# Hybrid decoder layer, down projection: banks copied by ScalarE, residual sums spread over the steps, activation combinations formed earlier; keys scaled once in the recurrence

## The chip, the cores and the metric

The kernel runs on one core of one Trainium2 chip. The metric is the device time of one launch in microseconds, as the median of several runs. One more execution is recorded by the hardware profiler; the views below come from that one.

## The reference

One layer of a hybrid decoder trunk, sequence 1024, model width 1024, all float32:

```python
h = rmsnorm(x, norm1_w)
proj = h @ w_in                       # q, k, v, z, beta, a for 4 gated DeltaNet heads; q, k, v for 8 dilated heads
o_a = gated_delta_rule(qa, ka, va, g, beta)   # per chunk: u = uv - wk@S; o = qd@S + at@u; S = ge*S + ke^T@u
o_b = dilated_attention(qb, kb, vb)
x = x + concat([rmsnorm(o_a) * silu(z), o_b]) @ w_out
u = causal_dwconv(rmsnorm(x, norm2_w) @ w_up, ffn_conv_w)      # width 3, 2 x 2816 columns
x = x + (silu(gate) * up) @ w_down    # 2816 -> 1024
return rmsnorm(x, final_norm_w)
```

In the state update the key is weighted: `k_end = kc * exp(gc[-1] - gc) * beta` (and in the kernel also by the norm of the key).

## The kernel before

Everything lies transposed: features on the 128 partitions, the 1024 tokens along the free axis. A float32 product is made of three matmuls (`mm3`, L183): each operand is split into a high part in the fp32r type and the rest (`split_block`, L1026: ScalarE copies the high part, VectorE subtracts it), and high x high, high x low and low x high are summed in a PSUM bank of 512 columns.

Engines work in order, each its own queue. The Python code is a set of streams (generators); `Weave.run` picks which stream goes on by a model of costs and due times, and the tile framework then orders the instructions of each engine and adds the semaphores. TensorE's order is fixed by a token (`mm`, L175); the other engines' instructions and the DMAs, all issued from SyncE, are placed by the framework's own schedule.

**Keys and the recurrence.** `kprep(h)` (L496) transposes the keys of head `h` to tokens (`ktok`), finds `bp` (beta over the squared norm) and `ke` (`bp` times the decay to the chunk's end), both per token. `chain(h)` (L704) runs over eight chunks of 128 tokens. In each, TensorE forms `w` (the corrected values) in columns P to 2P of a bank; VectorE copies it scaled by `ke` into `wke` (L742); ScalarE copies it unscaled into `w` (L743); TensorE forms `ktok^T wke` in columns 2P to 3P of the same bank (L746) and VectorE adds it to the state; `w` goes into the output product. The dense products of the input projection are woven between these small ones.

**Down projection.** The second MLP product is 2816 x 1024 on 1024 tokens. It is done by Strassen's scheme in Winograd's form with seven products instead of eight: the 22 feature tiles are two halves of `HT` = 11, the outputs two halves of 512 features (`mg`), the tokens two halves of 512 (`hh`). There are four stages of 11 steps (`STEPS`, L1335). A step of stages 0 to 2 makes two of the seven products for one pair of feature tiles: 4 output tiles x 3 matmuls into the banks `pa`, then the same into the banks `pb`, 24 matmuls of 128x512. Stage 3 makes the last product, into `pa` alone.

`prep(stage, j)` (L1253), called one step ahead, loads the raw weights (`wd`, `wa`) into two slots each of `wst` and `whi`, combines them on VectorE, combines the activations and splits all of them. The activations of a step are `R1[j]` (tokens 0 to 511 of both feature tiles) and `R2[j]` (tokens 512 to 1023), loaded from `upark`, where the up projection stored them. In the names of the scheme, T1 = q0 - r0, T2 = q1 - T1, T3 = q1 - q0 and T4 = r1 - T2, with r from `R1` and q from `R2`. Stage 0 forms T1, stage 1 forms T2 and T4, stage 2 forms T3. Splits go to a ring of eleven slots (`PTAGS`), four a step.

At the end of a stage (`j == HT - 1` in `down_step`, L1345) each bank is added by VectorE to the residual tile `x1h[m]`, for which the residual is loaded from `xpark` by `load_x1` (L1289) at the steps in `XLOADS`:

```python
ADDS = (((0, 0), (0, 0)), ((0, 1), (1, 1)), ((1, 1), (0, 1)))   # (mg, hh) of pa and of pb, by stage
```

A bank may be written by the next stage only after that. When a quarter of the output is whole, `complete` (L1307) squares it on ScalarE and VectorE sums the squares in `rstdB`; `final_norm` (L1316) sums over partitions with a product by ones, takes the inverse root on GpSimd, spreads it with a transpose, multiplies and stores. The tokens 0 to 511 of the last four tiles come at the very end, in halves of 256 columns (`last_product`, L1371).

The functions that the change touches:

Of the kernel before, what the change touches and what calls it, by code (L numbers as in the profile page):

```python
# [15 lines left out]
P = 128  # L16
# [118 lines left out]
def hybrid_layer(tc, I, out):  # L135
# [36 lines left out]
    def after(inst, anchor):  # L172
        tc.add_manual_dep(inst.ins, anchor.ins.name, order, reason="keeps a slot free until it is needed")
# [59 lines left out]
    def half(i):  # L233
        return slice(i * 512, i * 512 + 512)
# [261 lines left out]
    def kprep(h):  # L496
# [34 lines left out]
        ke = small("ke", 4)  # L531
        ve.tensor_tensor(ke, bp, eg, op=OP.mult)

# [14 lines left out]
        d.update(kT=kT, dec=dec, ge=ge, nk=nk, bp=bp, ke=ke, um=um)  # L548
# [155 lines left out]
    def chain(h):  # L704
# [5 lines left out]
        kT, ktok, vtok, yt, ge, rq, gq, ke = [d[n] for n in ("kT", "ktok", "vtok", "yt", "ge", "rq", "gq", "ke")]  # L710
# [8 lines left out]
        for c in range(NCH):  # L719
# [19 lines left out]
            w = tile_(sp, [P, P], F32, "w", "w" + tg, 1)  # L739
            if c < NCH - 1:  # L740
                wke = tile_(sp, [P, P], F32, "wke", "r" + tg, 1)
                ve.tensor_scalar(wke, ps[:, P:2 * P], ke[:, c:c + 1], None, op0=OP.mult)  # L742
            ac.activation(w, ps[:, P:2 * P], AF.Copy)  # L743
            if c < NCH - 1:
                yield wv.need(wke, slack=HOP)
                mm(ps[:, 2 * P:3 * P], ktok[:, cs], wke, 0.215)  # L746
                sn = sts[:, c % 2, :]
                if c == 0:
                    ve.tensor_copy(sn, ps[:, 2 * P:3 * P])
                else:  # L750
                    ve.scalar_tensor_tensor(sn, st, ge[:, c:c + 1], ps[:, 2 * P:3 * P], op0=OP.mult, op1=OP.add)
# [274 lines left out]
    def split_block(b, src):  # L1026
        ac.activation(b[0], src, AF.Copy)
        ve.tensor_tensor(b[1], src, b[0].bitcast(F32), op=OP.subtract)
# [191 lines left out]
    LAST = 5  # L1220

# [14 lines left out]
    def split_pair(src):  # L1236
# [4 lines left out]
        split_block((hi[0], lo[0]), src)  # L1241
        return [(hi[0][:, i, :], lo[0][:, i, :]) for i in range(2)]
# [10 lines left out]
    def prep(stage, j):  # L1253
        if stage == 0:

            g = raw_tile("wd", ("wst", "whi")[j % 2], wd_rows(j, 0))
            r = R1[j] = acts("r1", R1TAGS[j], j, 0)
            ops[stage, j] = list(zip(split_pair(g), split_pair(r)))
            q = R2[j] = A("r2", R2TAGS[j], shape=(P, 2, 512))
            sy.dma_start(q[:, 0, :], upark[j][:, half(1)])  # L1260
            ve.tensor_tensor(r[:, 0, :], q[:, 0, :], r[:, 0, :], op=OP.subtract)
        elif stage == 1:
# [4 lines left out]
            sy.dma_start(q[:, 1, :], upark[HT + j][:, half(1)])  # L1267
            t2 = tile_(wp, [P, 512], F32, "t2", "wlo", 2)
            ve.tensor_tensor(u[:, 1, :], u[:, 0, :], u[:, 1, :], op=OP.add)
            ve.tensor_tensor(u[:, 0, :], u[:, 1, :], a[:, 0, :], op=OP.subtract)  # L1270
            ve.tensor_tensor(t2, q[:, 1, :], r[:, 0, :], op=OP.subtract)
            w = split_pair(u)
            ops[stage, j] = [(w[0], split_one(t2)), (w[1], split_one(r[:, 0, :]))]
            ve.tensor_tensor(r[:, 1, :], r[:, 1, :], t2, op=OP.subtract)
        elif stage == 2:
# [3 lines left out]
            ve.tensor_tensor(g, g, u, op=OP.subtract)  # L1279
# [8 lines left out]

    def load_x1(mg, hh):  # L1289
        for m in range(4 * mg, 4 * mg + 4):  # L1290
            if not hh:
                x1h[m] = A("x1h", ("kT", "kT", "dv", "dv", "Xa", "Xa", "Xa", "Xa")[m])
            sy.dma_start(x1h[m][:, half(hh)], xpark[m][:, half(hh)])

# [12 lines left out]
    def complete(m, hh, sl):  # L1307
# [4 lines left out]
        ac.activation(sq[:, sl] if m else rstdB[:, sp_], x, AF.Square)  # L1312
        if m:
            ve.tensor_tensor(rstdB[:, sp_], rstdB[:, sp_], sq[:, sl], op=OP.add)

    def final_norm(hh, sl, tags, between=None):  # L1316
        n_ = (sl.stop - sl.start) // P
        ss = bank(tags[0])
        for c in range(n_):
            o = 512 * hh + sl.start + c * P  # L1320
            mm(ss[:, c:c + 1], rstdB[:, o:o + P], ones[:, :1], 0.215)
# [12 lines left out]

    STEPS = [(s_, j) for s_ in range(4) for j in range(HT)]  # L1335
    XLOADS = {6: (0, 0), 12: (1, 0), 14: (0, 1), 16: (1, 1)}

    ADDS = (((0, 0), (0, 0)), ((0, 1), (1, 1)), ((1, 1), (0, 1)))

    def mlp_down():  # L1340
# [20 lines left out]
        for n, (stage, j) in enumerate(STEPS):  # L1361
            if n + 1 < len(STEPS):
                prep(*STEPS[n + 1])
            if n in XLOADS:
                load_x1(*XLOADS[n])
# [5 lines left out]
        def last_product(i, sl):  # L1371
# [3 lines left out]
            complete(4 + i, 0, sl)  # L1375
# [7 lines left out]
        for i in (2, 3):  # L1383
            last_product(i, right)
        final_norm(0, right, ("hf", "ch"))
# [74 lines left out]
```

## Time and profile before

| | |
|---|---|
| median of 3 runs | 1264.93 us (1262.06 to 1266.37) |
| the profiled execution's own time | 1266.99 us |
| its span, first to last instruction | 1265.1 us, granted clock 0.990 |
| TensorE busy | 1241.6 us (98%) |
| VectorE busy | 940.8 us (74%) |
| ScalarE busy | 619.1 us (49%) |
| HBM traffic over the span | 117 GB/s |
| first to last down matmul starts | 1035.6 to 1253.6 us |

PE is TensorE's matmuls, PEld its weight loads, DVE VectorE, ACT ScalarE, POOL GpSimd, SP the queue that issues the DMAs. A timeline row gives start and length in us, engine, line, operation, out<-in, how many instructions are merged, and in brackets the engine's idle time before it with what ended it. A row of waits gives total us, times, longest. As nearly every operation passes through a helper, the line is nearly always L131 (or L176 for a matmul, L180 for a transpose), so groups are told apart by tile names: `pr` is a split operand, `r` is `R1` or `R2`, `wd` raw down weights, `dw` a bank of the down projection, `x1h` a residual tile.

### The profile page before, as it was taken

What the parts mean: (1) busy time and instruction counts of PE and PEld (TensorE: products, weight loads), DVE (VectorE), ACT (ScalarE), POOL (GpSimd) and SP (SyncE); (2) the same over time, 40 slices, a digit from 0 to 9 for tenths busy, and PEclk for the clock granted to TensorE, in tenths of its full rate; (3) what the DMA queues carried; (4) which work ended last, traced back from release to release, by engine and by line L of the source; (5) the groups of instructions that cost most, each with busy time, mean ns of one, the idle gap of its engine ahead of it and who ended that gap; (6) DMA issues with size and microseconds to landing.
All of it is one profiled execution on the core that took longest, in us unless ns stands there. A gap on an engine that the chain in (4) does not pass through costs nothing.

```text
span 1265.1 us, 18365 instructions
## 1 busy us (share of the span) xinstructions
PE 1241.6 (98%) x7070; PEld 1009.2 (80%) x7070; DVE 940.8 (74%) x1466; ACT 619.1 (49%) x1178; POOL 45.0 (4%) x34
## 2 busy tenths in 40 slices
PE   9999999999999999999999999999999999999996
PEld 7878887888676777878888888888888888787886
DVE  7485984573545456666888988988988989899975
ACT  7355544363666375455554444444445444343541
POOL 0012010022000000000000000000000000000000
PEclk9899999999999999999999999999999999999998
DMA  6112243335413321344312123122123198445623
GB/s 225 34 54 57 107 129 106 134 121 198 141 60 106 113 84 43 126 150 150 117 67 100 64 87 100 59 91 100 57 94 100 52 350 305 143 157 193 198 83 134
DMA packets 77767, 151.42 MB, mean 120 GB/s; under 512 B 21744, under 2 KB 28528, under 8 KB 77680
## 3 DMA queue, kind: packets, MB, share of 16 engines
q1 hardware_dynamic: 77680, 150.25, 35.4%
q8 instruction: 55, 0.90, 0.3%
q14 instruction: 32, 0.26, 0.1%
HBM read 112.21 MB, written 35.91 MB: 117 GB/s over the span
## 4 chain that ended last, share of the span: by engine, by line
PE 84%; DVE 6%; DMA 4%; issue 2%; ACT 2%; SPq 1%; POOLq 0%; POOL 0%; DVEq 0%; ACTq 0%
PE ps L176 42%; PE pa L176 19%; PE dw L176 11%; PE pc L176 9%; PE ps L180 4%; DMA wd<-in_wd 1%; DVE pr L131 1%; DVE kT L131 1%; DVE x1h L131 1%; DMA xt<-in_xT 1%; DMA wst<-in_w 1%; SPq L131 1%; DVE wd L131 1%; DMA wst<-in_wu 0%; DVE xr L131 0%
## 5 line engine op out<-in xcount | busy, mean ns | idle before, releaser
L176 PE MATMUL dw<-pr 128*128 128x512 f32 (+1 forms) x984 | 213.7, 377 | 3.2 <-DVE x1h L131 3.0
L176 PEld LDWEIGHTS dw<-pr 128*128 128x128 f32 x984 | 176.0, 188 | 39.8 <-DVE x1h L131 4.9
L176 PE MATMUL ps<-xhi,whi 128*128 128x512 f32 x448 | 188.2, 420 | 2.0 <-DVE xr L131 2.0
L176 PE MATMUL ps<-xhi,wlo 128*128 128x512 f32 x448 | 176.9, 395 | 0.6 <-DVE wlo L131 0.6
L176 PE MATMUL ps<-xlo,whi 128*128 128x512 f32 x448 | 176.6, 394 | 0.0
L176 PE MATMUL pa<-T,pair 128*128 128x512 f32 x528 | 128.7, 393 | 0.8 <-ACT u L131 0.8
L176 PEld LDWEIGHTS pa<-T,pair 128*128 128x128 f32 x528 | 100.1, 190 | 22.1 <-ACT u L131 1.1
L176 PEld LDWEIGHTS ps<-xhi,whi 128*128 128x128 f32 x448 | 85.3, 190 | 21.2 <-issue 5.1
L176 PEld LDWEIGHTS ps<-xhi,wlo 128*128 128x128 f32 x448 | 85.1, 190 | 19.7 <-DVE wlo L131 1.0
L176 PEld LDWEIGHTS ps<-xlo,whi 128*128 128x128 f32 x448 | 85.5, 191 | 13.5
L131 ACT ACTIVATE sm<-sm,mx 128x512 f32<-128x512 f32 (+2 forms) x128 | 79.6, 648 | 23.5 <-DVE mx L131 23.5
L131 ACT ACTIVATE u<-pa 128x512 f32<-128x512 f32 x44 | 26.3, 598 | 110.7 <-PE pa L176 110.7
L131 DVE SCALAR_TENSOR_TENSOR y<-xu,fcw,y 128x1023 f32<-128x1023 f32 (+1 forms) x44 | 56.3, 1281 | 25.7 <-ACT y L131 25.6
L131 ACT ACTIVATE whi<-wst 128x1024 fp32r<-128x1024 f32 (+2 forms) x38 | 38.6, 1017 | 66.1 <-PE ps L176 57.9
L176 PE MATMUL pc<-B,pair 128*128 128x512 f32 x264 | 63.4, 389 | 0.0
L176 PE MATMUL pa<-B,A 128*128 128x512 f32 x264 | 63.4, 389 | 0.0
L176 PE MATMUL pc<-T,S 128*128 128x512 f32 x264 | 63.4, 389 | 0.0
L176 PE MATMUL pa<-T,S 128*128 128x512 f32 x264 | 63.4, 389 | 0.0
L131 DVE TENSOR_TENSOR wst<-wst 128x512 f32<-128x512 f32 x88 | 60.4, 686 | 0.8
L176 PE MATMUL ps<-B,pair 128*128 128x512 f32 x252 | 60.5, 389 | 0.0
L131 ACT ACTIVATE pr<-wd 128x1024 fp32r<-128x1024 f32 x33 | 34.9, 1058 | 50.3 <-DVE wd L131 27.8
L176 PEld LDWEIGHTS pc<-B,pair 128*128 128x128 f32 x264 | 49.5, 188 | 10.3
(229 smaller groups left out, 2286.8 us busy)
## 6 DMA issues: line engine op xcount, KB each, us to landing
wst<-in_wu SPq DMA_DIRECT2D x44, 512.0 KB, 3.6
wd<-in_wd SPq DMA_DIRECT2D x44, 512.0 KB, 3.9
wst<-in_wi SPq DMA_DIRECT2D x25, 512.0 KB, 3.6
upark<-y SPq DMA_DIRECT2D x22, 512.0 KB, 3.5
apark<-aqkv SPq DMA_DIRECT2D x12, 512.0 KB, 2.9
r<-upark SPq DMA_DIRECT2D x11, 512.0 KB, 7.8
r<-upark SPq DMA_DIRECT2D x22, 256.0 KB, 6.7
wa<-in_wd SPq DMA_DIRECT2D x22, 256.0 KB, 2.7
```

Source lines behind the costliest of these rows:

```text
L131: return getattr(eng, op)(*a, **kw)
L176: tc.stamp_issue_order_token(nc.tensor.matmul(dst, lhs, rhs, start=start, stop=stop, **kw).ins, TOKEN)
L180: tc.stamp_issue_order_token(nc.tensor.transpose(dst, src, ident).ins, TOKEN)
```

## The change

In the recurrence, `kprep` scales the first seven chunks of `ktok` in place by `ke` on ScalarE (28 copies of 128x128 in all). In `chain` the scaled copy `wke` is gone; `w` is copied by VectorE instead of ScalarE, and this one copy feeds both the state product and the output product.

In the down projection:

- At the ends of stages 0 and 1 ScalarE copies each bank into `x1h` (`copy_to`) instead of VectorE adding it. The residual is loaded into tiles `res` of two output tiles each (`load_res`) and added later, one sum to a step (`add_res`), as is the sum of the two stage 0 products (`add_half`; the second one is now held in the `x1h` tiles of the other half), and the squares of the first four tiles (`square`). A table `JOBS` says at which step each stands. At the end of stage 2 VectorE adds as before.
- Each of those sums is ordered after the low part of the latest weights (`in_turn`), and the first combination of raw weights after the low part of the previous ones (`weight_sum`); these are orders on one engine, not waits.
- `R2[j]` is loaded whole in stage 0, and T3 formed there; for steps from `LATE` = 5 on, T4 is formed in stage 0 too, by another route. T2 is formed in place in stage 1 after T1 is split.
- In the last `final_norm`, the squares of the last two tiles are given to the product by ones as parts of their own, instead of being added to `rstdB` first.

The core of the diff:

```diff
-        ke = small("ke", 4)
+        ke = small("ke")
         ve.tensor_tensor(ke, bp, eg, op=OP.mult)
+        for c in range(NCH - 1):
+            ac.activation(v8(d["ktok"])[:, c, :], v8(d["ktok"])[:, c, :], AF.Copy, scale=ke[:, c:c + 1])
...
             w = tile_(sp, [P, P], F32, "w", "w" + tg, 1)
+            ve.tensor_copy(w, ps[:, P:2 * P])
             if c < NCH - 1:
-                wke = tile_(sp, [P, P], F32, "wke", "r" + tg, 1)
-                ve.tensor_scalar(wke, ps[:, P:2 * P], ke[:, c:c + 1], None, op0=OP.mult)
-            ac.activation(w, ps[:, P:2 * P], AF.Copy)
-            if c < NCH - 1:
-                yield wv.need(wke, slack=HOP)
-                mm(ps[:, 2 * P:3 * P], ktok[:, cs], wke, 0.215)
+                yield wv.need(w, slack=HOP)
+                mm(ps[:, 2 * P:3 * P], ktok[:, cs], w, 0.215)
...
+    def weight_pair(src):
+        pair, wlast[0] = split_pair(src, True)
+        return pair
+    def weight_sum(*a, **kw):
+        inst = ve.tensor_tensor(*a, **kw)
+        if wlast[0] is not None:
+            after(inst, wlast[0], "raw weights are released before the next ones are waited for")
...
         if stage == 0:
             g = raw_tile("wd", ("wst", "whi")[j % 2], wd_rows(j, 0))
             r = R1[j] = acts("r1", R1TAGS[j], j, 0)
-            ops[stage, j] = list(zip(split_pair(g), split_pair(r)))
-            q = R2[j] = A("r2", R2TAGS[j], shape=(P, 2, 512))
-            sy.dma_start(q[:, 0, :], upark[j][:, half(1)])
+            ops[stage, j] = list(zip(weight_pair(g), split_pair(r)))
+            q = R2[j] = acts("r2", R2TAGS[j], j, 1)
             ve.tensor_tensor(r[:, 0, :], q[:, 0, :], r[:, 0, :], op=OP.subtract)
+            ve.tensor_tensor(q[:, 0, :], q[:, 1, :], q[:, 0, :], op=OP.subtract)
+            if j >= LATE:
+                ve.tensor_tensor(r[:, 1, :], r[:, 1, :], q[:, 1, :], op=OP.subtract)
+                ve.tensor_tensor(r[:, 1, :], r[:, 1, :], r[:, 0, :], op=OP.add)
         elif stage == 1:
...
-            sy.dma_start(q[:, 1, :], upark[HT + j][:, half(1)])
-            t2 = tile_(wp, [P, 512], F32, "t2", "wlo", 2)
-            ve.tensor_tensor(u[:, 1, :], u[:, 0, :], u[:, 1, :], op=OP.add)
+            weight_sum(u[:, 1, :], u[:, 0, :], u[:, 1, :], op=OP.add)
             ve.tensor_tensor(u[:, 0, :], u[:, 1, :], a[:, 0, :], op=OP.subtract)
-            ve.tensor_tensor(t2, q[:, 1, :], r[:, 0, :], op=OP.subtract)
-            w = split_pair(u)
-            ops[stage, j] = [(w[0], split_one(t2)), (w[1], split_one(r[:, 0, :]))]
-            ve.tensor_tensor(r[:, 1, :], r[:, 1, :], t2, op=OP.subtract)
+            w = weight_pair(u)
+            t1 = split_one(r[:, 0, :])
+            ve.tensor_tensor(r[:, 0, :], q[:, 1, :], r[:, 0, :], op=OP.subtract)
+            ops[stage, j] = [(w[0], split_one(r[:, 0, :])), (w[1], t1)]
+            if j < LATE:
+                ve.tensor_tensor(r[:, 1, :], r[:, 1, :], r[:, 0, :], op=OP.subtract)
         elif stage == 2:
...
-            r = R2[j]
-            ve.tensor_tensor(r[:, 0, :], r[:, 1, :], r[:, 0, :], op=OP.subtract)
-            ops[stage, j] = list(zip(split_pair(g), split_pair(r)))
+            ops[stage, j] = list(zip(weight_pair(g), split_pair(R2[j])))
...
+    def load_res(mg, hh, i):
+        m = 4 * mg + i
+        t = res[m, hh] = tile_(wp, [P, 2, 512], F32, "res", "wlo", 2)
+        sy.dma_start(t, xpark[m:m + 2].rearrange("e p t -> p e t")[:, :, half(hh)])
+    def in_turn(*a):
+        after(ve.tensor_tensor(*a, op=OP.add), wlast[0], "the next step's weights go first")
+    def add_res(m, hh):
+        x = x1h[m][:, half(hh)]
+        in_turn(x, x, res[m - m % 2, hh][:, m % 2, :])
+    def add_half(m):
+        x = x1h[m][:, half(0)]
+        in_turn(x, x, x1h[4 + m][:, half(0)])
+    def copy_to(pd, m, hh):
+        ac.activation(x1h[m][:, half(hh)], pd, AF.Copy)
...
-    def final_norm(hh, sl, tags, between=None):
+    def final_norm(hh, sl, tags, between=None, more=()):
...
+        parts = [rstdB[:, o:o + n_ * P]] + list(more)
+        for i, t in enumerate(parts):
+            for c in range(n_):
+                mm(ss[:, c:c + 1], t[:, c * P:(c + 1) * P], ones[:, :1], 0.215, i == 0 and c == 0,
+                   i == len(parts) - 1, skip_group_check=True)
...
-    XLOADS = {6: (0, 0), 12: (1, 0), 14: (0, 1), 16: (1, 1)}
-    ADDS = (((0, 0), (0, 0)), ((0, 1), (1, 1)), ((1, 1), (0, 1)))
+    ADDS = (((0, 0), (1, 0)), ((0, 1), (1, 1)), ((1, 1), (0, 1)))
+    JOBS = {6: [(take_x1, 0)], 8: [(take_x1, 1)], 12: [(load_res, 0, 0, 0)], 13: [(load_res, 0, 0, 2)],
+            15: [(add_res, 0, 0)], 16: [(add_res, 1, 0)], 17: [(add_res, 2, 0)], 18: [(add_res, 3, 0)],
+            19: [(add_half, 0), (load_res, 0, 1, 0)], 20: [(add_half, 1), (load_res, 0, 1, 2)], 21: [(add_half, 2)],
+            22: [(add_half, 3), (square, 0)], 23: [(square, 1), (load_x1, 1, 0)], 24: [(add_res, 0, 1)],
+            25: [(add_res, 1, 1), (load_res, 1, 1, 0)], 26: [(add_res, 2, 1), (square, 2)],
+            27: [(add_res, 3, 1), (load_res, 1, 1, 2)], 28: [(add_res, 4, 1)], 29: [(add_res, 5, 1), (square, 3)],
+            30: [(add_res, 6, 1)], 31: [(add_res, 7, 1)]}
...
-                        add_to(pds[i], 4 * mg + i, hh, whole)
-                        if stage == 0 and e == 1:
-                            complete(i, 0, whole)
+                        if stage < 2:
+                            copy_to(pds[i], 4 * mg + i, hh)
+                        else:
+                            add_to(pds[i], 4 * mg + i, hh, whole)
...
-        for i in (2, 3):
-            last_product(i, right)
-        final_norm(0, right, ("hf", "ch"))
+        final_norm(0, right, ("hf", "ch"), more=[last_product(i, right, True) for i in (2, 3)])
```

More of the change, by code (lines that the diff above doesn't have):

```diff
@@ L170, in hybrid_layer, with after @@
     order = mybir.DependencyInfo(mybir.DependencyClass.NoSync, mybir.DependencyReason.DATA)
-    def after(inst, anchor):
-        tc.add_manual_dep(inst.ins, anchor.ins.name, order, reason="keeps a slot free until it is needed")
+    def after(inst, anchor, reason="keeps a slot free until it is needed"):
+        tc.add_manual_dep(inst.ins, anchor.ins.name, order, reason=reason)
     def mm(dst, lhs, rhs, us, start=True, stop=True, **kw):
@@ L709, in chain @@
         d = G[h]
-        kT, ktok, vtok, yt, ge, rq, gq, ke = [d[n] for n in ("kT", "ktok", "vtok", "yt", "ge", "rq", "gq", "ke")]
+        kT, ktok, vtok, yt, ge, rq, gq = [d[n] for n in ("kT", "ktok", "vtok", "yt", "ge", "rq", "gq")]
         if not ct:
@@ L1312, in complete @@
         ac.activation(sq[:, sl] if m else rstdB[:, sp_], x, AF.Square)
+        if alone:
+            return sq[:, sl]
         if m:
-            ve.tensor_tensor(rstdB[:, sp_], rstdB[:, sp_], sq[:, sl], op=OP.add)
-    def final_norm(hh, sl, tags, between=None):
+            r = rstdB[:, sp_]
+            if turn:
+                in_turn(r, r, sq[:, sl])
+            else:
+                ve.tensor_tensor(r, r, sq[:, sl], op=OP.add)
+    def final_norm(hh, sl, tags, between=None, more=()):
         n_ = (sl.stop - sl.start) // P
         ss = bank(tags[0])
-        for c in range(n_):
-            o = 512 * hh + sl.start + c * P
-            mm(ss[:, c:c + 1], rstdB[:, o:o + P], ones[:, :1], 0.215)
+        o = 512 * hh + sl.start
+        parts = [rstdB[:, o:o + n_ * P]] + list(more)
[3 more added lines that the diff above has]
+                   i == len(parts) - 1, skip_group_check=True)
         rs = tile_(sp, [P, 4], F32, "rs3", "rs3", 2)
```

34 lines of the change are left out of this document (21 added, 13 removed).

## The prediction

> **What bounds it now.** I read the page first, then the windows by stage, then who waited for whom in the down projection, then the timelines around each idle stretch of TensorE. The page's first part:
> ```profile
> PE 1241.6 (98%) x7070; PEld 1009.2 (80%) x7070; DVE 940.8 (74%) x1466; ACT 619.1 (49%) x1178; POOL 45.0 (4%) x34
> ```
> TensorE's own work does not change except for two 128x1 products in the last norm. So the change can only win what lies between matmuls and behind the last one, and lose by putting new holes there. Windows (us; PE, PEld, DVE, ACT, POOL busy with counts; granted clock; DMA share; GB/s), cut at starts of matmuls around the two ends of stages 0 and 1:
> ```profile
> 1035.57:1053.14 17.57, 17.34 (x75) 13.73 (x74) 16.75 (x18) 11.00 (x12) 0.00 (x0) 1.00 1.05 391
> 1096.00:1103.97 7.97, 6.33 (x24) 3.96 (x23) 7.97 (x13) 4.30 (x7) 0.00 (x0) 1.00 0.67 195
> 1103.97:1160.68 56.71, 56.71 (x251) 46.92 (x250) 52.41 (x74) 22.45 (x30) 0.00 (x0) 1.00 0.56 190
> 1160.68:1165.72 5.04, 3.72 (x15) 2.47 (x14) 5.04 (x8) 2.64 (x3) 0.00 (x0) 1.00 0.35 110
> 1165.72:1222.00 56.28, 56.28 (x250) 46.56 (x249) 48.17 (x57) 26.00 (x34) 0.00 (x0) 1.00 0.52 172
> ```
> A count includes the one already running at the cut. Third row: 250 matmuls start in 56.71 us, 0.2268 us each; a step of 24 is 5.44 us. Second row: 23 x 0.2268 = 5.22 us of work took 7.97, a loss of 2.75. Fourth: 14 x 0.2268 = 3.18 took 5.04, a loss of 1.86. First: 74 x 0.2268 = 16.78 took 17.57, a loss of 0.79. The long rows between lose nothing. VectorE is busy through both ends of a stage (7.97 of 7.97, 5.04 of 5.04). Who waited, 1035 to 1235:
> ```profile
> ACT pr L131 <- PE dw L176: 47.2, 20, 4.1
> DVE wd L131 <- DMA wd<-in_wd: 13.0, 13, 2.5
> PE dw L176 <- DVE x1h L131: 3.0, 6, 0.8
> ```
> and one of those six holes:
> ```profile
> 1096.98 1.22 DVE L131 TENSOR_TENSOR pr<-wd,pr 128x1024 fp32r<-128x1024 f32 x1
> 1098.12 0.68 DVE L131 TENSOR_TENSOR x1h<-x1h,dw 128x512 f32<-128x512 f32 x1
> 1098.72 0.68 DVE L131 TENSOR_TENSOR pr<-t,pr 128x512 fp32r<-128x512 f32 x1
> 1098.85 0.96 PE L176 MATMUL dw<-pr 128*128 128x512 f32 x3 [0.61 <-DVE x1h L131]
> ```
> The next stage may not write a bank until VectorE has added it to the residual, and that add stands in VectorE's queue behind the split of later weights.
>
> **Ends of stages 0 and 1: -4.3 us.** After the change ScalarE copies the eight banks of each end, at the price of
> ```profile
> L131 ACT ACTIVATE u<-pa 128x512 f32<-128x512 f32 x44 | 26.3, 598 | 110.7 <-PE pa L176 110.7
> ```
> about 0.6 us, against one bank finished every 3 x 0.2268 = 0.68 us. The built order puts the copies between splits for later steps. The one to fear is a split waiting for TensorE to free its slot (47.2 us in 20 waits above), but those at the head of the copies need slots that step 8 frees, two steps earlier. A bank has the other four (2.72 us) before it is written again, so a copy of 0.6 us has 2.1 to spare. Gain 4.61 at most, nothing if ScalarE stands blocked; I take 4.3.
>
> **VectorE in stage 0.** Each step gets the subtraction that had stood in stage 2 (11 operations of 128x512), steps 5 to 10 two more (12): 23. Stage 1 loses the late group's final subtraction; residual sums come one to a step. In all 6 more operations of 128x512. Prices, from start to start:
> ```profile
> 1036.39 1.22 DVE L131 TENSOR_TENSOR xu<-xu,rstdB 128x1024 f32<-128x1024 f32 x1 [3.32 <-ACT xu L131]
> 1037.53 1.22 DVE L131 TENSOR_TENSOR pr<-r,pr 128x1024 fp32r<-128x1024 f32 x1
> 1038.67 0.68 DVE L131 TENSOR_TENSOR xg<-u,pc 128x512 f32<-128x512 f32 x1
> 1039.26 1.28 DVE L131 SCALAR_TENSOR_TENSOR y<-xu,fcw,y 128x1023 f32<-128x1023 f32 x1
> 1040.46 1.22 DVE L131 TENSOR_TENSOR xg<-xg,rstdB 128x1024 f32<-128x1024 f32 x1
> ```
> L (128x1024) 1.14 us, S (128x512) 0.60, the convolution's 1.20. Walk along the new queue from 1036.39. To the last split of step 3: 8 L, 5 S, 3 convolutions = 15.7, so 1052.1. Before, that split ran here and held TensorE up:
> ```profile
> 1051.54 1.22 DVE L131 TENSOR_TENSOR pr<-r,pr 128x1024 fp32r<-128x1024 f32 x1
> 1052.81 2.56 PE L176 MATMUL dw<-pr 128*128 128x512 f32 x10 [0.23 <-DVE pr L131]
> ```
> So 0.4 of the 0.79 goes (0 to 0.6). To the last split of step 8: 11 L, 19 S, 1 convolution = 25.1, so 1077.3, and step 8 starts at 1052.3 + 5 x 5.44 = 1079.5: 2.2 to spare, the least of the walk. To the last of step 10: 3 L, 5 S, so 1083.7 against 1090.4. To step 11's: 1 L, 12 S, 1092.0, but its operand is split behind ScalarE's copies of the first two banks, done near 1092.4, so near 1093.6 against 1095.8. The 13.8 us put into stage 0 are thus covered by waits VectorE had there, and cost TensorE up to 23 x 0.60 less that cover if it is gone.
>
> Stages 0 to 2 as a whole: 66 L and 135 S, less 3 L and 2 S done before 1036.39, plus 3 L, 1 S and 4 convolutions left of the up projection: 160.4 us. TensorE needs 33 x 5.44 = 179.5, so 18.3 are free; the waits for weights took 13.0.
>
> The Trainium skill (VectorE: DVE Perf Modes, The DRAIN you can't avoid) says that the next operation does not start until the pipe has emptied, and advises to minimise their count. By it each operation would cost its full duration, and added ones would bite. The rows above disagree: durations of 1.22, next starts 1.14 later.
>
> **DMA queue.** Pairs of 256 KB loads of the activations become one of 512 KB, and twelve of 256 KB of the residual become six of 512 KB, the first ahead of the activations of step 1. At 391 GB/s (first window) that is 1.3 us later for what arrived here:
> ```profile
> 1034.81 1.06 ACT L131 ACTIVATE pr<-r 128x1024 fp32r<-128x1024 f32 x1 [5.51 <-DMA r<-upark]
> 1071.14 0.80 SPq L131 DMA_DIRECT2D r<-upark  x2
> DMA to landing us min/median/max: 2.6/7.2/9.2
> ```
> Step 1 starts at 1041.0, so it is covered. The last activations, issued at 1071.14, stand behind fewer loads now, near 1066; their first use is at 1073.1 in my walk, ahead of step 8's split. Landing after 9.2 us would be 1075.7, 2.6 late, 0.4 more than the spare. I take 0 (0 to +2).
>
> **The recurrence: -2.3 us.** Waits between 230 and 300, the worst place, and the price of the scaling:
> ```profile
> ACT w L131 <- DVE wke L131: 7.7, 8, 3.2
> PE ps L176 <- ACT w L131: 2.8, 4, 1.2
> 276.69 0.60 DVE L131 TENSOR_SCALAR wke<-ps,ke 128x128 f32<-128x128 f32 x2
> 277.18 1.04 ACT L131 ACTIVATE whi<-wst 128x1024 fp32r<-128x1024 f32 x1
> 278.12 0.42 ACT L131 ACTIVATE w<-ps 128x128 f32<-128x128 f32 x2
> 278.43 0.38 PE L176 MATMUL ps<-wke,ktok 128*128 128x128 f32 x1 [1.17 <-ACT w L131]
> L131 DVE TENSOR_SCALAR wke<-ps,ke x28: 340/349/353, 237.6 to 296.3; 128x128 f32<-128x128 f32 x28
> ```
> VectorE's scaled copy was done at 277.29; TensorE then waited for ScalarE's second read of the same bank, queued behind a split. The new VectorE copy stands where the scaling stood and is all that TensorE waits for. 28 scalings of 0.35 become 32 copies, four more: 1.4 us of an engine that is not full here. Of 2.8, one hole of 0.47 goes only in part: 2.3 (0 to 2.8). The planner's costs shift some groups of three dense matmuls (0.68 us) in this stage and in attention: 0, with -0.7 to +0.7.
>
> **Keys by token: 0.** 28 small copies on ScalarE, seven a head, at 1.14 / 4 = 0.29 us (first row), 2.0 a head:
> ```profile
> 109.42 1.14 ACT L131 ACTIVATE dec<-ps,ngc 128x128 f32<-128x128 f32 x4 [3.77 <-PE ps L180]
> 118.33 1.06 ACT L131 ACTIVATE whi<-wst 128x1024 fp32r<-128x1024 f32 x1 [0.69 <-PE ps L176]
> 120.16 1.15 ACT L131 ACTIVATE qT<-xr,gcw 128x1024 f32<-128x1024 f32 x1 [0.77 <-DVE xr L131]
> 118.32 0.17 DVE L131 TENSOR_TENSOR ke<-bp,eg 128x8 f32<-128x8 f32 x1
> 122.80 3.90 DVE L131 SCALAR_TENSOR_TENSOR qT<-xr,gcw,qT 128x1023 f32<-128x1023 f32 x3
> ```
> The third head's fall into the idle 3.77 us. The last head's wait for the factor at 118.49 and run to 120.5, so the weights split behind them ends 2.1 us later, and the query's first product at 122.5; VectorE takes it up at 122.80. Covered; without that cover +2.
>
> **Tail: -0.7 us.**
> ```profile
> 1253.90 0.74 DVE L131 TENSOR_TENSOR x1h<-x1h,dw 128x256 f32<-128x256 f32 x2
> 1254.41 0.75 ACT L131 ACTIVATE sq<-x1h 128x256 f32<-128x256 f32 x2 [3.38 <-DVE x1h L131]
> 1254.86 0.95 DVE L131 TENSOR_TENSOR rstdB<-rstdB,sq 128x256 f32<-128x256 f32 x2 [0.21 <-ACT sq L131]
> 1255.96 0.72 PE L176 MATMUL ps<-ones,rstdB 128*128 128x1 f32 x4 [2.10 <-DVE rstdB L131]
> ```
> TensorE sums the last two squares itself: it starts on the second at its end, 1255.16, plus the same hop of 0.15, 1255.31 instead of 1255.96.
>
> **The sum** is -0.4 - 4.3 - 2.3 - 0.7 = -7.7 us. The profiled execution took 1266.99 us (span 1265.1 and 1.9 around it), so 1259.3 there; the median of the three runs is 2.1 lower, so 1257.2.
>
> **Rivals.** (a) The ends of stages keep their holes, because a ScalarE split waiting for a slot or for VectorE stands ahead of a copy; for it the 47.2 us, against it the slots named above. Left are recurrence and tail, -3.0: 1261.9. (b) The recurrence keeps its holes, VectorE now being late with the copy behind long operations such as those it runs beside it; against it, the scaling it replaces was done 1.1 us before TensorE started. -5.4: 1259.5. (c) Slower: VectorE becomes the bound of stages 0 to 2. If operations cost their full durations (1.22, 0.69, 1.28) the 160.4 become 178.1, and with the 13.0 of waits 191, 12 us over TensorE, where 5.4 are lost now (2.75 + 1.86 + 0.79): +6.6, less recurrence and tail, +3.6: 1268.5. It decides once waits and slower starts eat the 18.3 us. The starts quoted above speak against it. The rule on the drain in the Trainium skill (VectorE: DVE Perf Modes) would bring it about. (d) The holes close, but TensorE meets as much waiting in the next step, the queues being in order: no change, 1264.9.
>
> **Chances.** Forecast 0.60, a 0.13, b 0.13, c 0.08, d 0.06. A measurement here tells 0.3% (3.8 us) from no change, so faster means below 1261.1: the forecast, b and a little of a, 0.76; the rest of a and d 0.15; slower 0.09. Range: all gains at their ends give -0.6 - 4.6 - 2.8 - 0.7 - 0.7 = -9.4, 1255.5, less 1 for the spread of runs, 1254.5; upwards to 1263.5, which holds a and b and leaves out c and d.
>
> **What would show it.** Windows over the two ends of stages with no loss against 0.2268 a matmul; no wait of TensorE on the residual tiles before stage 2 ends; no wait of TensorE on ScalarE's w; 0.7 less between the last down matmul and the end. Wrong: TensorE waiting for VectorE's splits in stage 0 near step 8, or VectorE idle for activations there; (c) if such holes come step after step.

## The result, and the profile after

The changed kernel takes 1261.01 us (median of 9 runs, 1259.93 to 1263.38), the kernel before beside it 1265.27 us (9 runs, 1262.06 to 1266.48). The medians differ by 4.3 us. The recorded ratio of the runs, which is not simply that of the two medians, is 0.9972, 95% interval 0.9962 to 0.9982, or 3.5 us less (2.3 to 4.8). Forecast was 7.7 less. The profiled execution took 1263.38 us, span 1261.4.

The page's line of busy times after:

```profile
PE 1240.0 (98%) x7078; PEld 1008.1 (80%) x7078; DVE 943.9 (75%) x1474; ACT 630.4 (50%) x1190; POOL 45.5 (4%) x34
```

Nearly nothing moves there. The stages tell more. The windows are cut at the start of the first matmul of the down projection and of the 264th, 528th and 792nd after it, which is by stage (columns as in the prediction: us, then PE, PEld, DVE, ACT, POOL busy with counts, granted clock, DMA share, GB/s). Before:

```profile
1035.58:1096.61 61.03, 60.59 (x265) 49.24 (x264) 52.57 (x62) 26.22 (x29) 0.00 (x0) 1.00 0.68 241
1096.61:1158.88 62.27, 60.85 (x264) 49.35 (x265) 57.97 (x83) 26.40 (x37) 0.00 (x0) 1.00 0.58 191
1158.88:1220.63 61.75, 60.43 (x266) 49.39 (x264) 53.64 (x64) 27.36 (x35) 0.00 (x0) 1.00 0.52 168
```

After:

```profile
1032.93:1092.77 59.84, 59.84 (x266) 49.56 (x264) 56.56 (x69) 28.75 (x32) 0.00 (x0) 1.00 0.64 226
1092.77:1152.94 60.17, 60.17 (x265) 49.33 (x264) 53.01 (x75) 28.63 (x45) 0.00 (x0) 1.00 0.58 184
1152.94:1217.56 64.62, 62.00 (x265) 48.93 (x264) 58.62 (x70) 30.79 (x39) 0.00 (x0) 1.00 0.58 181
```

264 matmuls at 0.2268 us need 59.88 us. What a row has above that is TensorE's loss: 1.2, 2.4 and 1.9 us before (the ends of stages 0 and 1 lie about the cuts), and 0.0, 0.3 and 4.7 us after. The holes that the change was aimed at are closed, and almost the same sum stands in stage 2, where TensorE had lost nothing before except at its edge. Who waited in the whole down projection after the change (us in total, times, longest):

```profile
DVE pr L131 <- ACT pr L131: 15.1, 26, 2.0
PE dw L176 <- DVE pr L131: 2.4, 5, 0.8
```

TensorE waits for VectorE's splits and no longer for the residual tiles. VectorE does not wait for weights any more (13.0 us before); it waits for ScalarE's splits, 15.1 us in 26 waits. (TensorE's 2.4 us is only what the view counts as idle; from start to start it is 4.7.) One step of stage 2, with the rows of VectorE, ScalarE and TensorE:

```profile
1184.40 1.23 DVE L131 TENSOR_TENSOR pr<-wd,pr 128x1024 fp32r<-128x1024 f32 x1 [1.19 <-ACT pr L131]
1185.55 0.69 DVE L131 TENSOR_TENSOR x1h<-x1h,res 128x512 f32<-128x512 f32 x1
1186.15 1.22 DVE L131 TENSOR_TENSOR wd<-wd 128x1024 f32<-128x1024 f32 x1
1187.28 1.22 DVE L131 TENSOR_TENSOR pr<-r,pr 128x1024 fp32r<-128x1024 f32 x1
1188.42 0.69 DVE L131 TENSOR_TENSOR wd<-wd 128x512 f32<-128x512 f32 x1
1188.54 0.63 ACT L131 ACTIVATE pr<-r 128x512 fp32r<-128x512 f32 x1 [3.21 <-DVE pr L131]
1188.56 5.73 PE L176 MATMUL dw<-pr 128*128 128x512 f32 x24 [0.65 <-DVE pr L131]
1189.20 1.06 ACT L131 ACTIVATE pr<-wd 128x1024 fp32r<-128x1024 f32 x1
1189.20 0.69 DVE L131 TENSOR_TENSOR pr<-r,pr 128x512 fp32r<-128x512 f32 x1
1190.29 1.23 DVE L131 TENSOR_TENSOR pr<-wd,pr 128x1024 fp32r<-128x1024 f32 x1 [0.40 <-ACT pr L131]
```

Read it as a loop through two engines. VectorE splits a step's weights (1184.40); the residual sum is tied behind that (`in_turn`), and the next weights' difference too (`weight_sum`); then comes the split of activations that TensorE stands waiting for (1187.28, done 1188.50, TensorE goes on at 1188.56); then the weights' second sum; only with that can ScalarE copy the next weights' high part (1189.20), and only with that copy can VectorE split them (1190.29). The stretch is 1.15 + 0.60 + 1.13 + 1.14 + 0.78 + 1.09 = 5.89 us, against a step of 5.44 on TensorE. ScalarE has a second reason to be no earlier: its copy of activations (1188.54 to 1189.17), which waited for the same split of VectorE, ends within 0.1 us of VectorE's second sum. The expectation for the sums in the wait, below, says that five of eight steps took 5.89. From stage 2's first split of weights to its eleventh there are ten loops, and it is 5.83 or 5.89 in four of them. With one more operation of 0.60 it is 6.43 or 6.49 in two, and in two others VectorE waits for nothing and its own work makes 6.35. The first takes 6.65, as ScalarE is still copying banks, and one 5.47.

The recurrence, from a product near 210 us to the first of the up projection, before and after:

```profile
210.22:611.12 400.90, 396.52 (x2947) 311.01 (x2947) 229.74 (x508) 216.78 (x529) 15.85 (x9) 1.00 0.34 116
```

```profile
210.00:608.21 398.21, 395.05 (x2947) 310.95 (x2947) 228.90 (x512) 210.82 (x497) 16.34 (x9) 1.00 0.36 117
```

2.7 us less for the same 2946 products. The tail after:

```profile
1251.34 0.75 ACT L131 ACTIVATE sq<-x1h 128x256 f32<-128x256 f32 x2 [3.38 <-DVE x1h L131]
1251.81 1.05 PE L176 MATMUL ps<-ones,sq 128*128 128x1 f32 x8 [0.17 <-ACT sq L131]
```

TensorE takes the squares as they come. From the end of the last down matmul to the end of the span it is 10.6 us, 11.3 before.

### The profile page after: what moved, and what is told of

Read it like the earlier page. It is cut to its first block, busy times and chain, and to the rows that moved or that the text cites. A ratio compares the mean times of both kernels' runs of the same rounds, so it can differ in the third digit from the quotient of the medians.

```text
span 1261.4 us, 18370 instructions
## 1 busy us (share of the span) xinstructions
PE 1240.0 (98%) x7078; PEld 1008.1 (80%) x7078; DVE 943.9 (75%) x1474; ACT 630.4 (50%) x1190; POOL 45.5 (4%) x34
## 4 chain that ended last, share of the span: by engine, by line
PE 87%; DVE 6%; ACT 3%; issue 2%; DMA 1%; SPq 0%; POOLq 0%; POOL 0%; DVEq 0%; ACTq 0%
PE ps L176 43%; PE pa L176 19%; PE dw L176 12%; PE pc L176 9%; PE ps L180 4%; ACT pr L131 1%; DVE pr L131 1%; DVE wd L131 1%; DVE kT L131 1%; ACT sq L131 1%; DVE x1h L131 1%; DMA xt<-in_xT 0%; DMA wst<-in_wu 0%; DVE xr L131 0%; ACT xhi L131 0%
## 5 line engine op out<-in xcount | busy, mean ns | idle before, releaser
L131 ACT ACTIVATE pr<-r 128x512 fp32r<-128x512 f32 (+1 forms) x55 | 43.5, 797 | 54.4 <-DVE r L131 20.6
L176 PEld LDWEIGHTS pa<-T,S 128*128 128x128 f32 x264 | 49.6, 188 | 10.3
## 6 DMA issues: line engine op xcount, KB each, us to landing
r<-upark SPq DMA_DIRECT2D x22, 512.0 KB, 10.4
```

The lines of the kernel that those rows point to most:

```text
L131: return getattr(eng, op)(*a, **kw)
L176: tc.stamp_issue_order_token(nc.tensor.matmul(dst, lhs, rhs, start=start, stop=stop, **kw).ins, TOKEN)
```

## The experiments

All times are medians. The experiments ran in three groups, each with the kernel before beside it (1264.48, 1264.88 and 1262.74 us), and ratios are to that. The loss of a stage is its window less 59.88 us, as above; all runs lost under 0.3 us in stage 0 except the one of before's down projection.

### Fewer and more sums in stage 2

Without the eight sums:

```
-            22: [(add_half, 3), (square, 0)], 23: [(square, 1), (load_x1, 1, 0)], 24: [(add_res, 0, 1)],
-            25: [(add_res, 1, 1), (load_res, 1, 1, 0)], 26: [(add_res, 2, 1), (square, 2)],
-            27: [(add_res, 3, 1), (load_res, 1, 1, 2)], 28: [(add_res, 4, 1)], 29: [(add_res, 5, 1), (square, 3)],
-            30: [(add_res, 6, 1)], 31: [(add_res, 7, 1)]}
+            22: [(add_half, 3), (square, 0)], 23: [(square, 1), (load_x1, 1, 0)],
+            25: [(load_res, 1, 1, 0)], 26: [(square, 2)],
+            27: [(load_res, 1, 1, 2)], 29: [(square, 3)]}
```

> The changed kernel with one thing left out: the eight residual sums of steps 24 to 31 (128x512, 0.60 us each on VectorE from start to start); the output then lacks the residual in its second half. Their loads stay. In the changed kernel VectorE's split of stage 2's weights came every 6.10 us on the average of eight steps (1160.20 to 1208.97), where TensorE needs 5.44, and TensorE lost about 4.7 us in seven holes. T1 (VectorE's load per step in stage 2: 3 of 1.14, 3 of 0.60 and about 0.4 of waiting for ScalarE, and a square's sum in some steps): without the sum a step is about 5.5 or less, the holes shrink to under 0.7 us in all, time 1261.0 - 4.3 = 1256.7. T2 (not the load, but the tie of the weights' first sum behind the last weight split, which makes VectorE wait for ScalarE 0.4 us a step): those ties are still here, so part of the holes stays, 1259. T3 (the residual's loads, that weights stand behind): loads unchanged, 1261.

Measured: 1257.68 us, ratio 0.9944 (0.9925 to 0.9963). Stage 2:

```profile
1149.89:1211.16 61.27, 60.77 (x265) 49.24 (x264) 53.82 (x62) 30.75 (x39) 0.00 (x0) 1.00 0.55 173
```

Loss 1.4 us in place of 4.7. The loads stayed, so they are not the cause (T3 falls). Each sum twice:

```
     def add_res(m, hh):
         x = x1h[m][:, half(hh)]
         in_turn(x, x, res[m - m % 2, hh][:, m % 2, :])
+        if hh:
+            in_turn(x, x, res[m - m % 2, hh][:, m % 2, :])
```

> The changed kernel with each of the eight residual sums of steps 24 to 31 done twice (the output then has the residual twice in its second half): 8 x 0.60 = 4.8 us more for VectorE in stage 2. T1 (load): every added us is lost by TensorE, as VectorE is already behind from step 24 on: holes 4.7 + 4.8 = 9.5, 1261.0 + 4.8 = 1265.8 (1264.5 to 1266.5). T2 (ties) and T3 (loads): the added sums fall into VectorE's waits for ScalarE (0.4 us a step) at least in part, 1262 to 1263.

Measured: 1265.14 us, ratio 1.0003 (0.9988 to 1.0018).

```profile
1150.86:1219.64 68.78, 63.38 (x266) 50.14 (x265) 62.47 (x77) 30.66 (x38) 0.00 (x0) 0.98 0.55 165
```

Loss 8.9, so 4.2 more for 4.8 us of sums; some 1.6 of the 4.2 are matmuls at a lower clock after a hole (last section). Both runs say that the sums are what costs. They do not say whether it is VectorE's amount of work or the place of the sums in its queue.

### Without the ties

No order constraint at all, and (second kernel, the first part of the diff alone) none for the weights:

```
     def weight_sum(*a, **kw):
         inst = ve.tensor_tensor(*a, **kw)
-        if wlast[0] is not None:
-            after(inst, wlast[0], "raw weights are released before the next ones are waited for")
...
     def in_turn(*a):
-        after(ve.tensor_tensor(*a, op=OP.add), wlast[0], "the next step's weights go first")
+        ve.tensor_tensor(*a, op=OP.add)
```

> The changed kernel without its order constraints: the weights' first sum, the residual sums and the squares' sums are no longer tied behind the last split of weights, so the scheduler places them. The work is the same. T1 (load): VectorE has as much to do in stage 2, so holes of about the same sum, 1261 (1260 to 1263). T2 (ties): VectorE's 0.4 us waits for ScalarE are filled, stage 2's holes shrink to under 1.5 us, 1257.5. T3 (loads): 1261.

> The changed kernel without the tie of the weights' first sum behind the last weight split; the residual and squares' sums stay tied. If that tie is what keeps VectorE from standing at a weight load that has not landed (13.0 us in 13 waits before, none in the changed kernel, 18.8 in 16 without either tie), those waits come back and with them holes in stages 1 and 2 of 5 to 10 us, 1268 (1265 to 1271). If only the sums' own tie matters, the time stays at 1261.

Measured: 1270.16 us, ratio 1.0043 (1.0028 to 1.0057), and 1271.62 us, 1.0062 (1.0039 to 1.0085). VectorE in the first and in the second:

```profile
DVE wd L131 <- DMA wd<-in_wd: 18.8, 16, 2.5
```

```profile
DVE wd L131 <- DMA wd<-in_wd: 24.3, 15, 3.3
```

TensorE lost 11.4 and 3.0 us in stages 1 and 2 of the first, 8.6 and 9.3 in the second. None of the three times for the first kernel came, and the second is just above its range. T2 as I had put it falls: the ties are no loss, the one of the weights keeps VectorE from standing at a weight load that has not landed. The prediction does not say that this tie is needed: without it the change is 6 to 9 us slower than before.

### Sums on GpSimd

```
     def in_turn(*a):
+        if late[0]:
+            po_.tensor_tensor(*a, op=OP.add)
+            return
...
         for n, (stage, j) in enumerate(STEPS):
...
+            late[0] = n >= 24
```

> The changed kernel with the eight residual sums and the two squares' sums of steps 24 to 31 on GpSimd, which is idle there (its product of 128x1024 took 1.92 us elsewhere in the kernel, so about 1 us for 128x512), all else in the same order. T1 (VectorE's load): holes of stage 2 gone, under 0.5 us, 1256.3. T2 (ties): as in the run without the sums, 1259. T3 (loads): 1261. A slowing of VectorE by GpSimd's work beside it would show as starts more than 1.14 apart, and would give back up to what was won.

Measured: 1266.99 us, ratio 1.0017 (1.0004 to 1.0031), over 10 us above the expectation of T1. VectorE while GpSimd ran four of the sums in a row from 1155.58:

```profile
1155.30 1.21 DVE L131 TENSOR_TENSOR pr<-wd,pr 128x1024 fp32r<-128x1024 f32 x1
1156.44 1.78 DVE L131 TENSOR_TENSOR x1h<-x1h 128x512 f32<-128x512 f32 x1
1158.14 2.28 DVE L131 TENSOR_TENSOR wd<-wd 128x1024 f32<-128x1024 f32 x1
1160.34 2.28 DVE L131 TENSOR_TENSOR pr<-r,pr 128x1024 fp32r<-128x1024 f32 x1
```

The run can't judge the theories, since the sums, now untied, ran in two bunches at the start of the stage, and VectorE's operations beside them took 2.28 us in place of 1.22 and 1.78 in place of 0.69. Over stages 1 and 2 VectorE was busy 116.2 us, against 106.8 in the kernel without the eight sums, which still has the two squares' sums: with the 1.2 us of those two, the ten sums on GpSimd took 10.6 us from VectorE, some 1.1 each, more than the 0.60 that a sum costs there. Stage 2 lost 10.9 us.

### Other work taken out of stage 2

The scheduler runs splits for stage 3 as early as stage 2. Five of them moved, then the squares of the first half and their sums as well:

```
-            ops[stage, j] = [(split_one(a[:, 0, :]), split_one(R1[j][:, 1, :], R2TAGS[j]))]
+            ops[stage, j] = [(split_one(a[:, 0, :]), split_one(R1[j][:, 1, :], R2TAGS[j], behind_r1(j)))]
+    def behind_r1(j):
+        return nlast[0] if j >= HT - LAST else None
...
-        split_block(b, src)
+        lo = split_block(b, src)
+        if behind is not None:
+            after(lo, behind)
...
-                ve.tensor_tensor(r, r, sq[:, sl], op=OP.add)
+                nlast[0] = ve.tensor_tensor(r, r, sq[:, sl], op=OP.add)
```

and in the second kernel besides, with the four `square` entries taken out of `JOBS`:

```
-                in_turn(r, r, sq[:, sl])
+                after(ve.tensor_tensor(r, r, sq[:, sl], op=OP.add), nlast[0])
...
-                final_norm(1, whole, ("hf", "ch"), lambda: down_step(stage, j))
+                final_norm(1, whole, ("hf", "ch"), lambda: (down_step(stage, j), [square(m) for m in range(4)]))
```

> The changed kernel with VectorE's low-part splits of stage 3's last five activations (128x512, 0.60 us each) tied behind the last sum of squares of the second half; in the changed kernel the scheduler runs four of them in the last steps of stage 2. The residual sums and their ties are as in the changed kernel. T1 (VectorE's load in stage 2, whatever it consists of): 4 x 0.60 = 2.4 us less to lose, holes 4.7 - 2.4 = 2.3, 1261.0 - 2.4 = 1258.6. T4 (it is the residual sums as such, through the buffers or banks that they wait for, not the load): no change, 1261. If the splits come too late for the last products of stage 3, a new hole after 1232 would show it.

> As the last, and the four squares of the first half and their three sums (0.60 us each) also moved from stage 2 behind the last sum of squares of the second half, where VectorE was idle for 2.8 and 3.1 us. T1: 7 x 0.60 = 4.2 us less for VectorE in stage 2, holes under 1 us, 1261.0 - 4.0 = 1257.0, the same as with the eight sums left out (1257.7), but with all the work done. T4: 1261. Risk: up to 1.8 us back if the moved sums delay the final norm of the second half.

Measured: 1260.64 us, ratio 0.9972 (0.9959 to 0.9984), and 1259.53 us, 0.9954 (0.9940 to 0.9968). Stage 2 of the first:

```profile
1150.54:1215.16 64.62, 62.12 (x265) 48.93 (x264) 55.74 (x65) 31.02 (x39) 0.00 (x0) 1.00 0.58 182
```

and of the second:

```profile
1152.19:1215.29 63.10, 61.69 (x265) 49.02 (x264) 54.10 (x63) 30.30 (x38) 0.00 (x0) 1.00 0.60 187
```

Against 64.62 and 58.62 of VectorE's work after the change, the first has 2.9 us less work in the stage and takes just as long: T1 in its plain form falls, and the time is that of T4. With 54.1 us of work the second still loses 3.2, while the kernel without the sums has 53.8 and loses 1.4. The first kernel's rows show why the splits cost nothing: they had stood in the wait for ScalarE, which is now 1.19 us where it was 0.40, and the loop is 5.89 as before.

```profile
1187.87 1.23 DVE L131 TENSOR_TENSOR pr<-wd,pr 128x1024 fp32r<-128x1024 f32 x1 [1.19 <-ACT pr L131]
1193.76 1.22 DVE L131 TENSOR_TENSOR pr<-wd,pr 128x1024 fp32r<-128x1024 f32 x1 [1.19 <-ACT pr L131]
```

In the second the sums are untouched and 1.5 us of loss go, which speaks against T4. The three loops that had held a square's sum are shorter: 5.28, 4.87 and 6.15 us for 5.89, 5.47 and 6.43. So the theory became T5: not the amount of work, but what stands in the loop.

### The same work, moved into the wait

```
             weight_sum(g, g, u, op=OP.subtract)
-            ve.tensor_tensor(g[:, 1, :], g[:, 0, :], g[:, 1, :], op=OP.add)
+            wsum[0] = ve.tensor_tensor(g[:, 1, :], g[:, 0, :], g[:, 1, :], op=OP.add)
...
     def in_turn(*a):
-        after(ve.tensor_tensor(*a, op=OP.add), wlast[0], "the next step's weights go first")
+        after(ve.tensor_tensor(*a, op=OP.add), wsum[0] or wlast[0], "the next step's weights go first")
```

and in the second kernel the moves of the last experiment as well.

> The changed kernel, the same work, with one tie changed: in stage 2 the residual sums and squares' sums stand behind the second sum of the next step's weights, where VectorE waits for ScalarE's split of them, and no longer behind the last split of weights. T5 (a loop in order: VectorE's split of weights 1.14, the sum tied behind it 0.60, the weights' difference 1.14, the split of activations that TensorE waits for 1.14, the weights' second sum to its end and the hop 0.78, ScalarE's split and the hop 1.09: 5.89 us from one weight split to the next, as measured in five of eight steps, against TensorE's 5.44; 6.49 with one more 0.60 in it): with the sum in the wait for ScalarE the loop is 5.29 and the holes of stage 2 (4.74 us in the changed kernel) shrink to under 1.0, 1261.0 - 4.0 = 1257.0. T1 (VectorE's load, whatever its order): as much work, holes of 4.7, 1261.

> Both together: sums in the wait for ScalarE as in the last run, the four squares and the five splits of activations moved behind the last sum of squares of the second half. T5: no hole is left in stage 2, under 0.5 us, 1256.5. T1: as with the moves alone (3.2 us of holes left, 1259.5).

Measured: 1255.70 us, ratio 0.9941 (0.9922 to 0.9960), and 1256.64 us, 0.9948 (0.9928 to 0.9967). Stage 2 of the first:

```profile
1151.78:1212.17 60.39, 60.13 (x265) 49.49 (x264) 56.79 (x69) 29.96 (x38) 0.00 (x0) 1.00 0.59 191
```

Loss 0.5 us, and of the second 0.5 too. The sum now stands where VectorE had waited:

```profile
1185.44 1.23 DVE L131 TENSOR_TENSOR pr<-wd,pr 128x1024 fp32r<-128x1024 f32 x1
1186.58 1.22 DVE L131 TENSOR_TENSOR wd<-wd 128x1024 f32<-128x1024 f32 x1
1187.72 1.22 DVE L131 TENSOR_TENSOR pr<-r,pr 128x1024 fp32r<-128x1024 f32 x1
1188.86 0.69 DVE L131 TENSOR_TENSOR wd<-wd 128x512 f32<-128x512 f32 x1
1189.46 0.69 DVE L131 TENSOR_TENSOR x1h<-x1h,res 128x512 f32<-128x512 f32 x1
```

The split of activations that TensorE needs follows the weights' split after 2.28 us, where it had been 2.88. VectorE's busy time in the window is 56.8 us, about 3 more than in the kernels that lose 1.4 and 3.2. T1 falls, and T4 as well: the sums and the tiles they use are the same. Not every loop is 5.29, though; the mean of the ten is 5.77. In two VectorE is busy throughout (6.96 and 6.36 us) and in one ScalarE is late (6.57). VectorE's work in the ten loops is 55.2 us, so there is little room left: TensorE needs 54.4. The time of the ten loops goes with the loss (each is 54.4, the loss and another 1.6 to 3.4 us; that VectorE's lead at the start of the stage covers this last part was not measured by itself):

| kernel | ten loops, us | loss in stage 2, us |
|---|---|---|
| changed | 61.3 | 4.7 |
| late splits moved | 60.8 | 4.7 |
| splits and squares moved | 59.3 | 3.2 |
| eight sums left out | 57.9 | 1.4 |
| sums in the wait | 57.7 | 0.5 |
| both | 57.0 | 0.5 |
| eight sums twice | 66.7 | 8.9 |

The two kernels without the tie of the weights do not follow this (61.4 and 60.3 us with 3.0 and 9.3 lost); there VectorE waits for loads.

The sums in the wait alone are the better version: about 7 us under the kernel before, about 4 under the changed one (0.9941 against 0.9972 of before, each in its own group), with the same work. Moving splits and squares as well brings nothing more.

### The parts alone

VectorE in place of ScalarE for the copies of banks:

```
-        ac.activation(x1h[m][:, half(hh)], pd, AF.Copy)
+        ve.tensor_copy(x1h[m][:, half(hh)], pd)
```

> The changed kernel with the copies of the sixteen banks at the ends of stages 0 and 1 made by VectorE in place of ScalarE, all else as it was. If it was VectorE's queue that held the banks, the holes at the two ends come back (2.75 and 1.86 us before, 4 to 6 here in all, since VectorE has 16 x 0.60 more to do), and stage 2 starts later: 1261 + 5 = 1266 (1264 to 1270). If the early sums of activations and the residual loads had closed the ends, nothing comes back: 1261 to 1262.

Measured: 1268.84 us, ratio 1.0043 (1.0028 to 1.0057). Stages 1 and 2, each with the end of the stage ahead of it:

```profile
1087.47:1151.55 64.08, 61.34 (x265) 49.32 (x264) 56.68 (x81) 23.34 (x33) 0.00 (x0) 1.00 0.54 174
1151.55:1219.53 67.98, 63.32 (x266) 50.19 (x265) 62.83 (x78) 30.64 (x38) 0.00 (x0) 0.97 0.54 173
```

Losses 4.2 and 8.1 in place of 0.3 and 4.7. The time came as forecast, but not in the forecast way. TensorE's waits in this down projection:

```profile
PE dw L176 <- DVE pr L131: 6.7, 7, 3.0
PE dw L176 <- ACT pr L131: 0.6, 2, 0.3
```

All are for splits, none is for a bank, and the matmuls of the first step after each end run without a hole. VectorE's copies came in time for the banks, and the splits that stood behind them came late. (Some 1.6 us of the 8.1 are matmuls at a lower clock after the hole of 3.0.) So VectorE had no room for the sixteen copies, but the run does not show what had held the banks before. That rests on the traces: six waits for `x1h` before, none after.

Last, the two halves of the change by themselves: before with the recurrence's part, and the changed kernel with before's recurrence (their diffs are the parts of the change shown at the start).

> The kernel before with one part of the change alone: keys by token scaled once, w copied by VectorE in the chains. C1 (ScalarE's second read was the wait): TensorE's four waits on ScalarE's w (2.8 us) go, nothing new of the same size comes: 1265 - 2.3 = 1262.7. C2 (the copy on VectorE is late too in some places, as in the changed kernel, where a wait of 0.92 us for VectorE stood at 276.7): half of it comes back, -1.2, 1263.8. The down projection is that of before: its holes of 2.75, 1.86 and 0.79 us stay.

> The changed kernel with the recurrence and the keys of before: the down projection's part of the change alone. T1 (what the ends of stages give, 5.4 us of holes, is paid back by VectorE's load in stage 2, about 4.7): from the first to the last down matmul 217.9 us as in the changed kernel against 218.3 before, and 0.6 from the tail: 1265 - 1.1 = 1263.9. If the parts add, this difference and that of the chains alone make up the -4.3 of the whole.

Measured: 1261.77 us, ratio 0.9977 (0.9963 to 0.9992), and 1262.66 us, 0.9986 (0.9971 to 1.0001), which can't be told from no change. The window of the recurrence with its part alone:

```profile
208.41:606.78 398.37, 395.25 (x2947) 310.99 (x2947) 228.90 (x512) 210.35 (x497) 16.32 (x9) 1.00 0.35 117
```

This is C1's outcome for the recurrence. The window is 398.4, and 400.9 again where before's recurrence runs in the changed kernel; the eleven other traces with the change's recurrence have 398.1 to 398.2. The down projection, first start to last end, is 217.8 us in the second kernel, 217.9 in the changed one and 218.3 before. So the recurrence is worth 2.5 to 2.7 us, the down projection 0.4, the tail 0.7: 3.8, between the 3.5 of the ratio and the 4.3 of the medians. The 0.4 is the least certain: before's down projection took 219.9 us in the trace of the recurrence's part alone, 1.6 more than in that of before.

## Why the prediction was wrong in size

**The step that failed** is the paragraph "Stages 0 to 2 as a whole", which set 160.4 us of VectorE's work against 179.5 of TensorE's, counted 18.3 us as free (the difference less the 0.8 us before VectorE's count starts) and went on with no price for stage 2. The work came out as said: operations still start 1.14 and 0.60 us apart. But time that is free in the sum of three stages was not free in the loop of one step. I walked VectorE's queue operation by operation through stage 0 alone. The same walk through one step of stage 2 would have needed one thing more, ScalarE's split between the weights' sum and VectorE's split of them (1.09 us with the hops), and the constraint `in_turn`, which puts the sum on the wrong side of it: 5.89 against 5.44. The sum lacked a term of +4.7; with it the forecast would have been -3.0, and the parts measured above add up to -3.8. VectorE also came into stage 2 with less in hand: its first split of weights there started 5.2 us ahead of TensorE's first product, 8.4 before the change.

**Ends of stages, -4.3, and the start, -0.4:** right, 5.1 for the two where 4.7 was forecast. Stages 0 and 1 lose 0.3 us after the change; the three rows before had lost 5.4. TensorE's waits for `x1h` are gone, which is the mechanism named. Which part of the edit did it is not shown: copies in place of sums, ScalarE in place of VectorE, and the earlier sums of activations came together, and with copies on VectorE no bank was late either. **VectorE in stage 0:** right, no loss there (0.0 us) though step 8 was to have only 2.2 us to spare. **DMA, 0:** right for TensorE; the activations' median landing on the page rose from 7.8 and 6.7 us (pairs and singles) to 10.4 without a hole.

**Recurrence, -2.3:** direction and place right, 2.7 measured, 0.4 more. The waits on ScalarE's `w` are gone. Not foreseen was a new one, on VectorE. It is like rival (b) in that VectorE's queue held a long split (1.23 us from 275.83), but it is not on the copy of `w`:

```profile
277.63 0.49 PE L176 MATMUL ps<-ct,qat 128*128 128x128 f32 x2 [0.92 <-DVE vtok L131]
```

TensorE's shown holes alone went down by about 1.6 us from 210 to 300; how the rest comes about between products with no shown idle time was not followed. **Keys, 0:** not settled. The first 210 us differ by up to 6 us between profiled executions (the mark lies at 205.0 to 211.1 us), more than the 2 us in question. **Tail, -0.7:** right, 0.7.

**Rivals.** The outcome is nearest to (d), "as much waiting", by its arithmetic, and to (c) by its engine, but neither named the place or the mechanism. (c) as priced did not come: it rested on operations costing their full durations, and after the change as before it the rows show less (1184.40, 1.23 long, next at 1185.55). The Trainium skill (VectorE: DVE Perf Modes, The DRAIN you can't avoid) says that the next operation waits for the empty pipe, but adds that one which is not held starts earlier; the trace agrees with the addition, which the prediction left out. VectorE became the bound with 6 us of idle time left in the stage. Had (d)'s sentence on queues in order been worked out for one step, its 0.06 would have been the main case.

## What to carry to other kernels

Add up the loop, not the engine: from one split of a step's weights to the next, through every queue it passes, hops included, and compare it with the bound engine's step; work that fits into a wait of the loop does not lengthen it, the same work in front of the wait lengthens it by its own duration (here 5.29 to 5.89 us). When operations are tied to an anchor to keep them out of the way, choose as anchor the last thing another engine is waiting for, so that they fall into the wait. A busy share or a sum over three stages does not show this: 18.3 us stood free in the sum, and stage 2 still lost 4.7.

## What the runs showed of the hardware beyond that

**TensorE's clock after a hole.** In the kernel with the sums twice TensorE stood from one start to the next for 2.76 us, and then (granted clock in the third column from the right):

```profile
1186.06:1188.82 2.76, 0.38 (x2) 0.00 (x0) 2.76 (x4) 0.02 (x1) 0.00 (x0) 1.00 0.53 174
1188.82:1192.69 3.87, 3.87 (x10) 2.99 (x11) 3.29 (x5) 2.62 (x3) 0.00 (x0) 0.59 0.77 237
```

About eight matmuls started 0.427 us apart in place of 0.227, some 1.6 us on top of the hole. So part of the 4.2 us that the doubled sums cost was this. The kernel without ties had a stop of 2.36 us with no such slowing behind it and stops of 2.66 and 2.95 with it. The Trainium skill (TensorE: Matmul & The Clock Gate, What's actually happening) puts the drop to half clock after an idle window of about 3.4 us that runs freely; here shorter stops were enough.

**GpSimd beside VectorE.** A sum of 128x512 on GpSimd took 2.0 us while VectorE worked:

```profile
L131 POOL TENSOR_TENSOR x1h<-x1h,res 128x512 f32<-128x512 f32 x8 | 15.9, 2011 | 523.3 <-ACT x1h L131 522.5 <-DMA res<-xpark 0.8
```

and lengthened each VectorE operation on two SBUF tiles beside it by 1.06 to 1.1 us. The Trainium skill (SBUF — State Buffer, Who interferes with whom) says that a VectorE instruction with two SBUF inputs contends with a GpSimd instruction that reads SBUF; the trace agrees, and an idle GpSimd was no free place for these sums.
